# The softmax reciprocals of an attention kernel, spread over partitions by four-row products with a 0/1 matrix in place of diagonal matrices

## The chip, the core and the metric

One core of one Trainium2 chip. The metric is the device time of one execution in microseconds (us); the figure given for a kernel is the median of its runs. Engines are named as the profile names them: PE (TensorE, with PEld its weight loads), DVE (VectorE), ACT (ScalarE), POOL (GpSimd) and SP (SyncE, which issues most DMAs).

## The reference, cut to what matters

One inference step of a one-layer encoder. A projection gives two branches. Branch A is a sparse attention over 2048 positions with 8 heads of 128; its output is multiplied by a gate and goes through two further matrix products with branch B and the residual.

```python
def sparse_attention(q, qi, wi, q_pos, k, v, ki, k_pos, topk):
    ...                                  # each query keeps its top-k admissible keys
    s = jnp.einsum('bqhgd,bqkhd->bqhgk', qg, kg).astype(jnp.float32) * (HEAD_DIM ** -0.5)
    s = jnp.where(valid[:, :, None, None, :], s, -jnp.inf)
    p = jax.nn.softmax(s, axis=-1).astype(v.dtype)
    o = jnp.einsum('bqhgk,bqkhd->bqhgd', p, vg)
    return o.reshape(B, Q, ATT_W)

a_out = (o * jax.nn.silu(za)) @ w_pa
...
merged = jax.nn.sigmoid(ga) * a_out + jax.nn.sigmoid(gb) * b_out
y = x + gate[:, None, :] * (merged @ w_out)
```

The softmax divides each query's row by its sum. The kernel does that after the product with V, where the result stands with the head's 128 channels on the partitions and the queries along the free axis, so that the reciprocal of each query's sum has to be had on every partition.

## The kernel before

The program has three stages in the profiled execution: the projections (matmuls L998 to L1000, until about 1773 us), the attention (`attention()`, about 1773 to 2324 us) and the output products (`outputs()`, from there to the end). The code writes the work of each stage down in one order, and a scheduler in the program's build sets the order of the instructions on each engine from its own estimate of the times. Wide matmuls are done in three passes of f32r (an f32 form that PE reads with reduced precision): a high part of each operand (ACT's cast in `split`, L193) and what is left of it (DVE's or POOL's subtraction, L194).

The attention goes over 16 blocks of 128 queries, in the order 4, 0, 5, 1, 6, 2, 7, 3, 8 to 15; block b reads (b+1) times 128 keys. Each block has four pairs of heads, so there are 64 pairs. `qk(pr)` makes the logits of a pair (L1402 to L1404 with the weights `khi`, `klo`), adds the mask and takes the maximum (DVE, L1413), then exponentials and their sums (ACT, L1418), then the reciprocals of the sums, `sc[:, 20:22]` (DVE, L1419), one column for each of the two heads, queries on partitions. `pv(pr)` is called three pairs later. It transposes the exponentials (PE, L1439, in a PSUM tile of `ptile()`, of which there are three buffers), splits them into `th` and `tl`, and multiplies with V into the first 256 columns of `po` (L1447 to L1449). `po` has one buffer here, the same that `psi` had in the stage before.

The reciprocals get onto all partitions in `pv` as well. POOL splits them into `rr` (L1428, L1429: two high parts and two remainders), and makes from them two diagonal matrices for each part, `dg` (L1432, two instructions of 128x256 a pair). PE multiplies these with a matrix of ones, `ones_r` (L1450, L1451: two products of 256 columns), into the other 256 columns of `po`. DVE multiplies the gate `z` with these columns (L1456) and the result with the first ones (L1457), POOL makes differences (L1459 to L1461), and `xa_d` is stored (L1462).

The last `pv` is followed by a flag: PE sums it (L1869), DVE casts it to `fi` (L1871), and SP reads it (L1874, TENSOR_LOAD). `outputs()` loads pieces of the two branches from `xb_d` and `xa_d` into `xq` (L1573, five buffers, 768 KB each), of the weights into `rw` (L1553), splits both (ACT L1535 makes `xh` and `wh`, DVE L1536 `xl` and `wl`), and multiplies (L1709 to L1711). Its pool for `xq` and `xl` takes memory that the pool `ke` of the attention had, in which `khi`, `klo` and the first mask stand; a load into it waits for the last reader of what stood there.

Of the kernel before, what the change touches and what calls it, by code (L numbers as in the profile page):

```python
# [9 lines left out]
F32 = mybir.dt.float32  # L10
F32R = mybir.dt.float32r
# [3 lines left out]
ALU = mybir.AluOpType  # L15
# [4 lines left out]
P = 128  # L20
# [86 lines left out]
def body(ctx, tc, x_prompt, x_sample, cache_k, cache_v, cache_idx_k, state_conv, c_prompt, c_sample,  # L107
# [3 lines left out]
    V, S, G, T = nc.vector, nc.scalar, nc.gpsimd, nc.tensor  # L111
# [5 lines left out]
    def nm(s):  # L117
        uid[0] += 1
        return f"{s}_{uid[0]}"
# [9 lines left out]
    cp = ctx.enter_context(tc.tile_pool(name="cp", bufs=1))  # L129
# [25 lines left out]
    ident = cp.tile([P, P], F32, name="ident")  # L155
    ones = cp.tile([P, P], F32, name="ones")
    V.memset(ones, 1.0)
    ones_r = cp.tile([P, P], F32R, name="ones_r")
    V.tensor_copy(ones_r, ones)
    half = cp.tile([P, 4], F32, name="half")  # L160
    V.memset(half, -0.5)
    vecs = cp.tile([P, 96], F32, name="vecs")
# [1129 lines left out]
    def attention(shared=None, aside=()):  # L1292
        aside = list(aside)
        sums = []
        with ExitStack() as p2:
            ke = p2.enter_context(tc.tile_pool(name="ke", bufs=1, reuse_waits="tile"))
            kp = p2.enter_context(tc.tile_pool(name="kp", bufs=1, reuse_waits="tile"))
            ap_ = p2.enter_context(tc.tile_pool(name="ap", bufs=2, reuse_waits="tile"))
# [10 lines left out]
            def ptile():  # L1309
                pts[0] += 1  # L1310
                return (px if pts[0] % 3 == 0 else pst).tile([P, 512], F32, name=nm("pt"), tag="pt")
# [4 lines left out]

            khi = ke.tile([P, 2, SEQ], F32R, name="khi")
            klo = ke.tile([P, 2, SEQ], F32R, name="klo")
            mks = [ke.tile([P, SEQ], BF16, name=nm("mk"), tag="mk0")]
            vhi = kp.tile([P, NB, 256], F32R, name="vhi")  # L1320
            vlo = kp.tile([P, NB, 256], F32R, name="vlo")
# [33 lines left out]
            def block(b):  # L1355
                L = P * (b + 1)
                r0 = b * P
                st = {}
# [23 lines left out]
                def qk(pr):  # L1382

                    if pr == 0 and not st:
                        prep()
                    sc = ap_.tile([P, 32], F32, name=nm("sc"), tag="sc", bufs=5)
                    g = pr // 2
                    sms = []
                    spare = count[0] % 3 == 2 and 6 < count[0] < 60 and shared is not None
                    count[0] += 1  # L1390
                    for i in range(2):
                        if spare:
                            sm = sp.tile([P, SEQ], F32, name=nm("s"), tag=("sc", "low")[i], bufs=2 - i)
                        else:
                            sm = ap_.tile([P, SEQ], F32, name=nm("s"), tag="s", bufs=6)
                        sms.append(sm)
                        qh, ql = [t[:, 2 * (pr % 2) + i, :] for t in st["q", g]]
                        ci = 0
                        for grp in groups:
                            ps = psq.tile([P, 2, 512], F32, name=nm("ps"), tag="ps")  # L1400
                            for k, (o, w) in enumerate(grp):
                                T.matmul(ps[:, k, :w], qh, khi[:, g, o:o + w], start=True, stop=False)  # L1402
                                T.matmul(ps[:, k, :w], qh, klo[:, g, o:o + w], start=False, stop=False)  # L1403
                                T.matmul(ps[:, k, :w], ql, khi[:, g, o:o + w], start=False, stop=True)  # L1404
                            o, w = grp[0]
                            if len(grp) == 2 and grp[1][1] == w:
                                ops = [(ps[:, :, :w], o, 2, w)]
                            else:
                                ops = [(ps[:, k:k + 1, :w], o, 1, w) for k, (o, w) in enumerate(grp)]
                            for src, o, nn, w in ops:  # L1410
                                out = sm[:, o:o + nn * w].rearrange("p (a b) -> p a b", a=nn)
                                mk = st["mk"][:, o:o + nn * w].rearrange("p (a b) -> p a b", a=nn)
                                V.tensor_tensor_reduce(out, src, mk, 1.0, -3.0e38 if ci == 0 else sc[:, i * 8 + ci - 1:i * 8 + ci], ALU.add, ALU.max, sc[:, i * 8 + ci:i * 8 + ci + 1])  # L1413
                                ci += 1
                        c1 = i * 8 + ci - 1
                        r = st["r"][:, 2 * pr + i:2 * pr + i + 1]
                        V.tensor_scalar(sc[:, 16 + i:17 + i], sc[:, c1:c1 + 1], r, -1.0, ALU.mult, ALU.mult)  # L1417
                        S.activation(sm[:, :L], sm[:, :L], AF.Exp, bias=sc[:, 16 + i:17 + i], scale=r, accum_out=sc[:, 18 + i:19 + i])  # L1418
                    V.reciprocal(sc[:, 20:22], sc[:, 18:20])  # L1419
                    st[pr] = (sms, sc)  # L1420

                def pv(pr):
                    sms, sc = st.pop(pr)
                    po = pso.tile([P, 512], F32, name=nm("po"), tag="pi")
                    g = pr // 2

                    rr = ap_.tile([P, 4], F32R, name=nm("rr"), tag="rr")
                    G.tensor_copy(rr[:, 0:2], sc[:, 20:22])  # L1428
                    G.tensor_tensor(rr[:, 2:4], sc[:, 20:22], rr[:, 0:2].bitcast(F32), ALU.subtract)  # L1429
                    dg = ap_.tile([P, 2, 256], F32R, name=nm("dg"), tag="dg")  # L1430
                    for k in range(2):
                        G.tensor_tensor(dg[:, k, :].rearrange("p (i q) -> p i q", i=2), ident.unsqueeze(1).to_broadcast([P, 2, P]),  # L1432
                                        rr[:, 2 * k:2 * k + 2].bitcast(F32).unsqueeze(2).to_broadcast([P, 2, P]), ALU.mult)
                    for j0 in range(0, nj, 2):
                        js = list(range(j0, min(j0 + 2, nj)))
                        pt = ptile()
# [7 lines left out]
                        for jj, j in enumerate(js):  # L1444
# [2 lines left out]
                            T.matmul(po[:, 0:256], vh_, th[:, pc], start=(j == 0), stop=False)  # L1447
                            T.matmul(po[:, 0:256], vh_, tl[:, pc], start=False, stop=False)  # L1448
                            T.matmul(po[:, 0:256], vl_, th[:, pc], start=False, stop=(j == nj - 1))  # L1449
                    T.matmul(po[:, 256:512], ones_r, dg[:, 0, :], start=True, stop=False)  # L1450
                    T.matmul(po[:, 256:512], ones_r, dg[:, 1, :], start=False, stop=True)  # L1451
                    hs = slice(2 * pr, 2 * pr + 2)
                    z = aq.tile([P, 256], F32, name=nm("z"), tag="z", bufs=3)
                    load(z.rearrange("p (h q) -> p h q", h=2), z_d[hs, :, r0:r0 + P].rearrange("h p t -> p h t"))
# [7 lines left out]
                    store(xa_d[pr, :, :, 64 * b:64 * b + 64].rearrange("s p t -> p s t"), ps_)  # L1462

                return prep, [(lambda pr=pr: qk(pr), lambda pr=pr: pv(pr)) for pr in range(4)]

            order = [4, 0, 5, 1, 6, 2, 7, 3, 8, 9, 10, 11, 12, 13, 14, 15]
# [371 lines left out]
    def general():  # L1838
# [26 lines left out]
        outputs()  # L1865

    attention((ip, pst, psi), gates + [conv_out])
    pf = pst.tile([P, 512], F32, name="pf", tag="pt")
    T.matmul(pf[:1, 0:1], flag, ones[:, 0:1], start=True, stop=True)  # L1869
# [93 lines left out]
```

## Time and profile before

| what | us |
|---|---|
| runs | 2834.89, 2835.08, 2839.24 |
| median | 2835.08 |
| profiled execution, its own time | 2831.79 |
| its span | 2829.9 |
| mean granted PE clock | 0.992 of full speed |

The span is what the profiler's records cover, from the first instruction to the last; the execution's own time has 1.9 us around it, and stands 3.3 us below the median. Busy times of matmuls overlap (they are pipelined), so the cost of a matmul on PE is read from the distance between starts, and a row with xN holds N instructions that follow each other. In forms of PE the words 128*128 are the rows and columns of the weights in use, the rest is what is moved through and written; types of PE are all shown as f32.

### The profile page before, as it was taken

To read this page: it belongs to the slowest core of one execution; us is meant where nothing else is said; L and a number is where in the kernel's file an instruction comes from. 1 tells how busy PE (TensorE), PEld (TensorE's weight loads), DVE (VectorE), ACT (ScalarE), POOL (GpSimd) and SP (SyncE) were. 2 spreads that over 40 slices of the span, in tenths; PEclk is the share of its full clock that TensorE was granted. 3 is DMA by queue.
4 is the path that set the end of the run, shared out by engine and by line. 5 is a ranking of instruction groups with operands and counts; after the bars stand their busy time and mean duration, and the time that the engine had idled before them with its cause. 6 is when DMAs were issued, how large, how long until landed. Compare 5 with 4: busy or idle time off the path is not lost. (4 is left out here: it accounts for less than half of the span.)

```text
span 2829.9 us, 51791 instructions
## 1 busy us (share of the span) xinstructions
PE 2730.2 (96%) x18206; PEld 2636.1 (93%) x18206; DVE 2203.2 (78%) x4549; ACT 1506.2 (53%) x2719; POOL 1030.5 (36%) x1430
## 2 busy tenths in 40 slices
PE   8998899999999999999999999899999999999998
PEld 6988899999999989999999999889999999999997
DVE  6676668577778898778887855898887769887988
ACT  4433655665666754534544433676665654454453
POOL 3342646455554243222342221577554430010100
PEclk9999899999999999999999999999999999999999
DMA  8578744455454676565776775677554459896885
GB/s 292 179 241 270 244 157 162 160 170 169 158 168 162 209 195 221 180 196 187 215 222 205 224 242 164 143 198 204 152 169 147 133 186 349 253 305 208 258 295 155
DMA packets 485841, 576.29 MB, mean 204 GB/s; under 512 B 179506, under 2 KB 375298, under 8 KB 484546
## 3 DMA queue, kind: packets, MB, share of 16 engines
q1 hardware_dynamic: 476706, 556.55, 62.5%
q0 software_dynamic: 4160, 12.06, 1.2%
q10 hardware_dynamic: 4704, 4.26, 0.4%
q8 instruction: 145, 2.38, 0.4%
q14 instruction: 126, 1.03, 0.1%
HBM read 379.83 MB, written 199.22 MB: 205 GB/s over the span
## 5 line engine op out<-in xcount | busy, mean ns | idle before, releaser
L998 PE MATMUL pm<-bh,wo 128*128 128x352 f32 (+1 forms) x2688 | 865.7, 323 | 11.4 <-DVE u L1097 3.0
L999 PE MATMUL pm<-bl,wo 128*128 128x352 f32 (+1 forms) x2688 | 864.2, 322 | 0.0
L1000 PE MATMUL pm<-bh,wo 128*128 128x352 f32 (+1 forms) x2688 | 860.9, 322 | 0.0
L998 PEld LDWEIGHTS pm<-bh,wo 128*128 128x128 f32 x2688 | 507.0, 189 | 20.0 <-DVE u L1097 3.7
L999 PEld LDWEIGHTS pm<-bl,wo 128*128 128x128 f32 x2688 | 507.5, 189 | 6.1 <-issue 0.9
L1000 PEld LDWEIGHTS pm<-bh,wo 128*128 128x128 f32 x2688 | 505.5, 188 | 4.2 <-issue 0.5
L194 POOL TENSOR_TENSOR wo<-wr,wo 128x512 fp32r<-128x512 f32 x160 | 226.7, 1418 | 669.4 <-ACT wo L193 645.7
L255 DVE SCALAR_TENSOR_TENSOR sc<-pi,wi,sc 128x512 f32<-128x512 f32 (+3 forms) x287 | 192.1, 671 | 55.2 <-ACT pi L251 51.0
L251 ACT ACTIVATE pi<-pi 128x512 f32<-128x512 f32 (+3 forms) x328 | 164.7, 517 | 127.9 <-PE pi L250 120.4
L1535 ACT CAST wh<-rw 128x1024 fp32r<-128x1024 f32 x128 | 134.2, 1052 | 171.0 <-PE ps L1710 76.5
L193 ACT CAST th<-pt 128x512 fp32r<-128x512 f32 (+1 forms) x288 | 154.7, 561 | 129.7 <-PE pt L1439 116.7
L1709 PE MATMUL ps<-xh,wh 128*128 128x384 f32 (+1 forms) x672 | 214.3, 321 | 2.0 <-ACT oa L1664 0.8
L194 DVE TENSOR_TENSOR tl<-pt,th 128x512 fp32r<-128x512 f32 (+1 forms) x288 | 184.0, 655 | 40.5 <-ACT th L193 39.7
L1710 PE MATMUL ps<-xl,wh 128*128 128x384 f32 (+1 forms) x672 | 214.4, 320 | 0.0
L1711 PE MATMUL ps<-xh,wl 128*128 128x384 f32 (+1 forms) x672 | 211.6, 320 | 0.5 <-DVE wl L1536 0.5
L1536 DVE TENSOR_TENSOR wl<-rw,wh 128x1024 fp32r<-128x1024 f32 x128 | 155.5, 1221 | 50.3 <-ACT wh L1535 50.3
L1418 ACT ACTIVATE s<-s,sc,rts 128x384 f32<-128x384 f32 (+15 forms) x128 | 166.2, 1298 | 48.3 <-DVE sc L1417 36.5
L318 ACT ACTIVATE low<-sc,w 32x1056 f32<-32x1056 f32 (+14 forms) x105 | 136.6, 1301 | 87.1 <-DVE w L323 86.2
L193 ACT CAST wo<-wr 128x512 fp32r<-128x512 f32 x160 | 98.4, 615 | 140.9 <-PE pm L999 109.0
L1790 POOL DMA_DIRECT2D out_dram<-om x60 | 31.7, 534 | 388.8 <-DVE om L1788 388.8
L1063 DVE TENSOR_TENSOR u<-u,pm 128x352 f32<-128x352 f32 (+1 forms) x240 | 122.1, 510 | 58.4 <-PE pm L1000 54.6
L1447 PE MATMUL po<-th,vhi 128*128 128x256 f32 x544 | 158.7, 292 | 6.6 <-DVE a L1457 2.6
(323 smaller groups left out, 7208.1 us busy)
## 6 DMA issues: line engine op xcount, KB each, us to landing
u<-u_d SPq DMA_DIRECT2D x128, 520.0 KB, 3.7
wr<-in_w_f_dram SPq DMA_DIRECT2D x96, 512.0 KB, 4.2
rw<-o_d SPq DMA_DIRECT2D x72, 512.0 KB, 5.9
u_d<-ev SPq DMA_DIRECT2D x192, 176.0 KB, 2.5
rw<-in_w_q_dram SPq DMA_DIRECT2D x56, 512.0 KB, 6.3
s_d<-ws SPq DMA_DIRECT2D x64, 256.0 KB, 3.0
wr<-s_d SPq DMA_DIRECT2D x32, 512.0 KB, 5.1
xa_d<-a SPq DMA_DIRECT2D x64, 256.0 KB, 3.2
```

Source lines behind the costliest of these rows:

```text
L193: S.copy(hi, src)
L194: (eng or V).tensor_tensor(lo, src, hi.bitcast(F32), ALU.subtract)
L251: S.activation(pi[:n, :w], pi[:n, :w], AF.Relu)
L255: V.scalar_tensor_tensor(sc[:n, o:o + w], pi[:n, :w], wi[:n, b, h:h + 1], sc[:n, o:o + w], ALU.mult, ALU.add)
L998: T.matmul(ps[:, :tb], wh[:, kt, :], bh[:, kt, :tb], start=(first and kt == 0), stop=False, **more)
L999: T.matmul(ps[:, :tb], wh[:, kt, :], bl[:, kt, :tb], start=False, stop=False, **more)
L1000: T.matmul(ps[:, :tb], wl[:, kt, :], bh[:, kt, :tb], start=False, stop=(kt == 3), **more)
L1418: S.activation(sm[:, :L], sm[:, :L], AF.Exp, bias=sc[:, 16 + i:17 + i], scale=r, accum_out=sc[:, 18 + i:19 + i])
L1447: T.matmul(po[:, 0:256], vh_, th[:, pc], start=(j == 0), stop=False)
L1709: T.matmul(ps[:, :tb], wh[:, kt, wc], xh[:, kt, :tb], start=(first and kt == 0), stop=False, **more)
L1710: T.matmul(ps[:, :tb], wh[:, kt, wc], xl[:, kt, :tb], start=False, stop=False, **more)
L1711: T.matmul(ps[:, :tb], wl[:, kt, wc], xh[:, kt, :tb], start=False, stop=(kt == 3), **more)
```

## The change

`ones_r` and the matrices `dg` go. A matrix `pick2` of zeros and ones is made once, in the pool `ke`: for head i, rows i and i + 2 are ones. The split of the reciprocals (`rr`, POOL) moves from `pv` to the end of `qk`. In `pv`, PE transposes `rr` (128 queries by 4) into four rows of 128 in a tile of `ptile()`, ACT copies these rows to `row`, and at the end of the pair two products of 128 columns, with the first four rows of `pick2` as weights and `row` moved through, write the other 256 columns of `po`: each adds the high part and the remainder of one head.

```diff
-    ones_r = cp.tile([P, P], F32R, name="ones_r")
-    V.tensor_copy(ones_r, ones)
...
+            pick2 = ke.tile([P, 2, P], F32R, name="pick2")
+            for i in range(2):
+                V.tensor_tensor(pick2[:, i, :], ident[:, i:i + 1].to_broadcast([P, P]), ident[:, i + 2:i + 3].to_broadcast([P, P]), ALU.add)
...
                     V.reciprocal(sc[:, 20:22], sc[:, 18:20])
-                    st[pr] = (sms, sc)
+                    rr = ap_.tile([P, 4], F32R, name=nm("rr"), tag="rr", bufs=6)
+                    G.tensor_copy(rr[:, 0:2], sc[:, 20:22])
+                    G.tensor_tensor(rr[:, 2:4], sc[:, 20:22], rr[:, 0:2].bitcast(F32), ALU.subtract)
+                    st[pr] = (sms, rr)
...
-                    rr = ap_.tile([P, 4], F32R, name=nm("rr"), tag="rr")
-                    G.tensor_copy(rr[:, 0:2], sc[:, 20:22])
-                    G.tensor_tensor(rr[:, 2:4], sc[:, 20:22], rr[:, 0:2].bitcast(F32), ALU.subtract)
-                    dg = ap_.tile([P, 2, 256], F32R, name=nm("dg"), tag="dg")
-                    for k in range(2):
-                        G.tensor_tensor(dg[:, k, :].rearrange("p (i q) -> p i q", i=2), ident.unsqueeze(1).to_broadcast([P, 2, P]),
-                                        rr[:, 2 * k:2 * k + 2].bitcast(F32).unsqueeze(2).to_broadcast([P, 2, P]), ALU.mult)
+                    pr_ = ptile()
+                    T.transpose(pr_[:4, 0:P], rr.bitcast(F32), ident)
+                    row = ap_.tile([P, P], F32R, name=nm("row"), tag="row")
+                    S.copy(row[:4], pr_[:4, 0:P])
...
-                    T.matmul(po[:, 256:512], ones_r, dg[:, 0, :], start=True, stop=False)
-                    T.matmul(po[:, 256:512], ones_r, dg[:, 1, :], start=False, stop=True)
+                    for i in range(2):
+                        T.matmul(po[:, 256 + P * i:384 + P * i], pick2[:4, i, :], row[:4], start=True, stop=True)
```

PE in the middle of the attention, at the end of one pair (po is the pair's result, dg the diagonal matrices, s the exponentials). Before:

```order
L1404 MATMUL ps_23084<-khi,ql_22797 128x384
L1450 MATMUL po_23108<-dg_23112,ones_r 128x256
L1451 MATMUL po_23108<-dg_23112,ones_r 128x256
L1439 MATMUL pt_23283<-ident,s_22890 128x128
L1439 MATMUL pt_23283<-ident,s_22906 128x128
```

The same pair after (line numbers are those of the changed kernel; row holds the four rows, pick_20211 is pick2):

```order
L1447 MATMUL po_23153<-th_23208,vhi 128x256
L1431 MATMUL pt_23308<-ident,rr_22963 4x128
L1448 MATMUL po_23153<-tl_23209,vhi 128x256
...
L1449 MATMUL po_23153<-th_23221,vlo 128x256
L1451 MATMUL po_23153<-row_23156,pick_20211 128x128 x2
L1439 MATMUL pt_23327<-ident,s_22930 128x128
```

The two products of a pair still stand next to each other, in all 64 pairs, between instructions that use all 128 rows; the transposition of `rr` is an instruction more.

SP where the attention ends and `outputs()` begins. Before:

```order
L1573 DMA xq_28243<-xb_d 128x4x384
L1454 DMA z_28197<-z_d 128x2x128
L1573 DMA xq_28259<-xb_d 128x4x384
L1573 DMA xq_28265<-xb_d 128x4x384
L1462 DMA xa_d<-a_27784 128x8x64
L1573 DMA xq_28357<-xb_d 128x4x384
L1573 DMA xq_28447<-xb_d 128x4x384
L1462 DMA xa_d<-a_27923 128x8x64
L1462 DMA xa_d<-a_28061 128x8x64
L1874 TENSOR_LOAD fi
```

After:

```order
L1454 DMA z_28262<-z_d 128x2x128
L1462 DMA xa_d<-a_27855 128x8x64
L1462 DMA xa_d<-a_27992 128x8x64
L1462 DMA xa_d<-a_28128 128x8x64
L1874 TENSOR_LOAD fi
L1874 ISA x2
L1573 DMA xq_28308<-xb_d 128x4x384
L1573 DMA xq_28324<-xb_d 128x4x384
L1573 DMA xq_28330<-xb_d 128x4x384
L1573 DMA xq_28422<-xb_d 128x4x384
L1462 DMA xa_d<-a_28264 128x8x64
L1573 DMA xq_28512<-xb_d 128x4x384
```

The first five loads of `xq` stood among the last pairs' transfers and ahead of the read of the flag; now they stand behind it, since `pick2` lies in the memory that they write and is read by the very last product of the attention.

PE at the same place, after:

```order
L1449 MATMUL po_28135<-th_28250,vlo 128x256
L1451 MATMUL po_28135<-row_28138,pick_20211 128x128 x2
L1709 MATMUL ps_28347<-xh_28319,wh_28310 128x384
L1709 MATMUL ps_28362<-xh_28319,wh_28310 128x384
L1709 MATMUL ps_28376<-xh_28319,wh_28314 128x384
L1709 MATMUL ps_28390<-xh_28319,wh_28314 128x384
L1710 MATMUL ps_28347<-xl_28320,wh_28310 128x384
```

Before, L1709, L1710 and L1711 took turns from the start; now four products that need only `xh` stand ahead of the first that needs `xl`.

## Rows read from the trace of the kernel before

**Rows 1.** The page's first part: busy time of each engine, share of the span, number of instructions.
```profile
PE 2730.2 (96%) x18206; PEld 2636.1 (93%) x18206; DVE 2203.2 (78%) x4549; ACT 1506.2 (53%) x2719; POOL 1030.5 (36%) x1430
```

**Rows 2.** Busy time by stretch: two of the attention, and the first two tens of us of the output stage. The columns: the stretch and its length, then busy us (and instructions) of PE, PEld, DVE, ACT, POOL, the granted PE clock, the share of DMA time, and GB/s.
```profile
1773.00:1933.00 160.00, 145.91 (x1023) 133.18 (x1024) 138.14 (x418) 108.00 (x230) 107.77 (x279) 0.99 0.69 176
1933.00:2290.00 357.00, 355.23 (x2570) 335.33 (x2568) 289.55 (x668) 221.52 (x336) 189.31 (x397) 1.00 0.57 162
2330.00:2340.00 10.00, 10.00 (x59) 10.00 (x58) 9.46 (x12) 6.88 (x10) 0.57 (x2) 1.00 1.00 366
2340.00:2350.00 10.00, 9.83 (x56) 9.24 (x54) 4.49 (x9) 4.58 (x6) 1.07 (x2) 1.00 1.04 390
```

**Rows 3.** PE in time around the end of one pair: start in us, duration, engine, line, operation, out<-in, weights' rows*columns, what is written, count.
```profile
1789.76 0.28 PE L1449 MATMUL po<-th,vlo 128*128 128x256 f32 x1
1789.87 0.28 PE L1450 MATMUL po<-dg,ones_r 128*128 128x256 f32 x1
1789.99 0.28 PE L1451 MATMUL po<-dg,ones_r 128*128 128x256 f32 x1
1790.11 0.38 PE L1439 MATMUL pt<-ident,s 128*128 128x128 f32 x2
```

**Rows 4.** POOL from 1773 to 2330 us, the diagonal matrices and the first half of the split of the reciprocals: count, then busy us, mean ns of one, idle time before and what ended it.
```profile
L1432 POOL TENSOR_TENSOR dg<-ident,rr 128x256 fp32r<-128x256 f32 x128 | 78.3, 630 | 89.2 <-PE po L1451 78.9 <-DMA wq<-in_w_q_dram 10.2
L1428 POOL CAST rr<-sc 128x2 fp32r<-128x2 f32 x64 | 12.4, 194 | 53.5 <-DVE sc L1419 52.9
```

**Rows 5.** PE in time, matmuls that use 32 of the 128 rows of the weights (L457) between matmuls that use all of them, in the projection stage.
```profile
1683.74 0.32 PE L998 MATMUL pm<-bh,wo 128*128 128x336 f32 x1
1683.99 0.48 PE L457 MATMUL po<-sm,sm 32*128 32x128 f32 x2
1684.40 0.42 PE L999 MATMUL pm<-bl,wo 128*128 128x336 f32 x1
1684.66 0.32 PE L1000 MATMUL pm<-bh,wo 128*128 128x336 f32 x1
1684.82 0.33 PE L998 MATMUL pm<-bh,wo 128*128 128x352 f32 x1
```

**Rows 6.** PE in time, two transpositions that use 4 rows (L566) among f32r products of 256 columns.
```profile
17.42 0.28 PE L560 MATMUL pm<-wh,cs 128*4 128x256 f32 x1
17.53 0.28 PE L561 MATMUL pm<-wl,cs 128*4 128x256 f32 x1
17.74 0.28 PE L566 MATMUL pm<-ident,row 4*128 4x4 f32 x2
17.96 0.28 PE L560 MATMUL pm<-wh,cs 128*4 128x256 f32 x1
```

**Rows 7.** PE's groups by line and form: two of 256 columns that differ in type (L556 f32, L560 f32r by their declarations). Count, busy us, mean ns of one, idle time before.
```profile
L560 PE MATMUL pm<-wh,cs 128*4 128x256 f32 x40 | 9.7, 279 | 0.0
L556 PE MATMUL pm<-x,cs 128*4 128x256 f32 x16 | 3.8, 379 | 0.0
```

**Rows 8.** PE in time, f32r products of 128 columns with all rows in use (the logits of the first block).
```profile
1793.99 0.27 PE L1403 MATMUL ps<-klo,qh 128*128 128x128 f32 x1
1794.10 0.28 PE L1404 MATMUL ps<-khi,ql 128*128 128x128 f32 x1
```

**Rows 9.** PE in time, a transposition whose weights have all 128 rows and 32 columns (L451).
```profile
1741.96 0.32 PE L1000 MATMUL pm<-bh,wo 128*128 128x336 f32 x1
1742.11 0.27 PE L451 MATMUL pt<-ident,box 128*32 128x128 f32 x1
1742.22 0.60 PE L1343 MATMUL pt<-ident,s 128*128 128x128 f32 x4
```

**Rows 10.** ACT, the nearest form to the copy of the four rows: count, busy us, mean ns.
```profile
L731 ACT ACTIVATE sq<-pm 128x128 bf16<-128x128 f32 x32 | 8.9, 277 | 24.1 <-PE pm L766 19.8 <-PE pt L208 2.0 <-DVE sm L738 1.9
```

**Rows 11.** PE's groups from 1773 to 1933 us with idle time before them (last column: us, and what ended it).
```profile
L1439 PE MATMUL pt<-ident,s 128*128 128x128 f32 x272 | 40.9, 277 | 3.9 <-DVE tl L194 3.3 <-DVE sc L1413 0.2
L1447 PE MATMUL po<-th,vhi 128*128 128x256 f32 x129 | 37.7, 292 | 4.6 <-DVE a L1457 2.2 <-DVE sc L1417 1.0 <-ACT khi L193 0.7
L1451 PE MATMUL po<-dg,ones_r 128*128 128x256 f32 x28 | 7.9, 282 | 0.0
```

**Rows 12.** The end of the attention in time on SP's queue (start, time until the last of the row's transfers, count), then on ACT, DVE and PE.
```profile
2291.62 0.36 SPq L1573 DMA_DIRECT2D xq<-xb_d  x1
2296.70 1.47 ACT L1535 CAST xh<-xq 128x1536 fp32r<-128x1536 f32 x1 [0.83 <-DMA xq<-xb_d]
2298.20 1.76 DVE L1536 TENSOR_TENSOR xl<-xq,xh 128x1536 fp32r<-128x1536 f32 x1 [2.13 <-ACT xh L1535]
2323.61 0.28 PE L1451 MATMUL po<-dg,ones_r 128*128 128x256 f32 x1
2323.73 0.33 PE L1709 MATMUL ps<-xh,wh 128*128 128x384 f32 x1
2323.90 0.34 PE L1710 MATMUL ps<-xl,wh 128*128 128x384 f32 x1
```

**Rows 13.** What PE waited for from 2290 to 2313 us: waiter, releaser, us in total, times, longest.
```profile
PE po L1448 <- DVE tl L194: 1.5, 1, 1.5
PE po L1447 <- ACT th L193: 1.5, 1, 1.5
```

More of the change, by code (lines that the diff above doesn't have):

```diff
@@ L1419, in qk @@
                     V.reciprocal(sc[:, 20:22], sc[:, 18:20])
-                    st[pr] = (sms, sc)
+                    rr = ap_.tile([P, 4], F32R, name=nm("rr"), tag="rr", bufs=6)
+                    G.tensor_copy(rr[:, 0:2], sc[:, 20:22])
+                    G.tensor_tensor(rr[:, 2:4], sc[:, 20:22], rr[:, 0:2].bitcast(F32), ALU.subtract)
+                    st[pr] = (sms, rr)
                 def pv(pr):
-                    sms, sc = st.pop(pr)
+                    sms, rr = st.pop(pr)
                     po = pso.tile([P, 512], F32, name=nm("po"), tag="pi")
                     g = pr // 2
-                    rr = ap_.tile([P, 4], F32R, name=nm("rr"), tag="rr")
-                    G.tensor_copy(rr[:, 0:2], sc[:, 20:22])
-                    G.tensor_tensor(rr[:, 2:4], sc[:, 20:22], rr[:, 0:2].bitcast(F32), ALU.subtract)
-                    dg = ap_.tile([P, 2, 256], F32R, name=nm("dg"), tag="dg")
-                    for k in range(2):
-                        G.tensor_tensor(dg[:, k, :].rearrange("p (i q) -> p i q", i=2), ident.unsqueeze(1).to_broadcast([P, 2, P]),
-                                        rr[:, 2 * k:2 * k + 2].bitcast(F32).unsqueeze(2).to_broadcast([P, 2, P]), ALU.mult)
+                    pr_ = ptile()
+                    T.transpose(pr_[:4, 0:P], rr.bitcast(F32), ident)
+                    row = ap_.tile([P, P], F32R, name=nm("row"), tag="row")
+                    S.copy(row[:4], pr_[:4, 0:P])
                     for j0 in range(0, nj, 2):
```

## The prediction

> **What bounds the kernel now.** The page's shares come first: PE is busy for 96% of the span, POOL for 36% [rows 1]. A share is a mean over stages, so the next view is the busy time by stretch [rows 2]. In the attention from 1933 to 2290 us PE is busy for 355.23 of 357 us: each tenth of a microsecond that PE gets or loses there is one of the kernel. From 1773 to 1933 us, where the small blocks are done, PE is busy for 145.91 of 160 and DVE for 138.14: PE waits now and then for DVE. So the change is judged by what it does to PE. POOL, which it relieves most, is no limit: its diagonal matrices wait for PE (the 78.9 us ended by L1451 are POOL's own idle time) [rows 4], never the other way round, since L1450 follows L1449 after 0.11 us and without idle time [rows 3].
>
> **What goes.** On POOL 128 matrices at 630 ns [rows 4], 78 us: worth nothing, since nobody waits for them; DVE's instructions do not become fewer by it. On PE the two products of 256 columns: L1450, L1451 and the next instruction start at 1789.87, 1789.99 and 1790.11 [rows 3], so the two take 0.24 us a pair.
>
> **What comes, on PE.** First the transposition of `rr`, with weights of 128 rows and 4 columns. The nearest row is a transposition with 128 rows and 32 columns, which starts 0.15 us after a product of 336 columns and is followed after 0.11 us [rows 9]: 0.11 us, with no gap on either side. The products L560 with 4 columns follow each other at 0.11 to 0.12 us too [rows 6]. I take 0.11.
>
> The Trainium skill, TensorEngine Tiling (Array Packing), Key Properties, says that a change of the tiling mode drains the array, and lists modes narrow in columns beside those narrow in rows. By that rule this transposition would pay the gaps as well; the row of L451 shows none at 32 columns, and the rival "drain at both" below has that time.
>
> Then the two products, which use only four rows of weights. This trace has no f32r product of that kind. Between which rows does it lie? The **upper end** is L457: 32 rows, 128 columns, in f32. At 1683.74 an L998 of 336 columns starts, then come two L457 and an L999, and at 1684.66 the L1000 starts: 0.92 us, of which the two neighbours need 0.15 or 0.16 each (L1000 to L998: 1684.66 to 1684.82). That leaves 0.61 us for the two, where two full-row products would take 0.22 [rows 5, 8]. So the few rows cost, not the columns: a gap on entering, on leaving, and no overlap between the two. The **lower end** is L566: 4 rows, 4 columns. From L561 at 17.53 to L560 at 17.96 there are 0.43 us; L561 itself takes 0.12, which leaves 0.31 for the two [rows 6]; they move nearly nothing, so 128 columns cost more. In between: f32 moves slower than f32r, 379 against 279 ns for 256 columns [rows 7], 0.05 us for 128. L457 less twice 0.05 is **0.51 us for two f32r products**, my estimate.
>
> A pair then takes 0.51 + 0.11 instead of 0.24: **+0.38 us** (ends: 0.31 + 0.11 - 0.24 = +0.18, and +0.48). From 1933 us on there are 64 - 28 = 36 pairs (28 L1451 until then) [rows 11] on an engine without idle time: 36 x 0.38 = 13.7 us. Of the 28 before, I let a fifth go into the 14 us that PE stands anyway: 28 x 0.38 x 0.8 = 8.5. Together **+22.2 us** (ends +10.5, and +30.7 with nothing absorbed).
>
> **What comes beside PE.** ACT gets 64 copies of 4x128, at most 277 ns each [rows 10]: 18 us, where it is busy for 330 of 517 us [rows 2], off the path. But the transposed rows hold one of three PSUM tiles until ACT has copied them, 64 more users beside the tiles of exponentials; PE already waits 3.3 us for such tiles and 2.2 us for the single `po` [rows 11], and the order after leaves somewhat less PE work between a pair's products and the next pair's first L1447. For both **+2 us** (0 to 4). The two instructions for `pick2` replace one cast, once: nothing. `rr` moves from `pv` to `qk` in the code alone: POOL's idle time before L1428 is ended by the reciprocals already (52.9 of 53.5 us) [rows 4], so it does them as soon as they are there. Nothing.
>
> **The end of the attention.** SP's five loads of `xq` pass behind the flag's read and behind the last product. Before, the first was issued at 2291.62 and its split began at 2296.70, 5.08 us later; `xh` took 1.47, `xl` 1.76, long before L1709 at 2323.73, which followed the last product after 0.12 us [rows 12]. Now the load goes out when the last product is done: 5.1 + 1.5 + 1.8 = 8.4 us until the first L1710, in which only four L1709 at 0.17 us fit: PE stands for **7.7 us**. Given back are the waits of 1.5 + 1.5 us in the last pairs [rows 13]: there `xh` and `xl` sat ahead of `th` and `tl` on ACT and DVE [rows 12], and they do so no longer. Net **+4.7 us**.
>
> **Sum.** 22.2 + 2 + 4.7 = +28.9 us on the profiled execution: 2831.8 + 28.9 = 2860.7. The median stands 3.3 us above that execution: **2864 us**. Its own range by the ends of the price: +10.5 + 2 + 4.7 = +17 to +30.7 + 2 + 4.7 = +37, which is 2852 to 2872.
>
> **Rivals.**
> *Few rows cost nothing extra.* The four-row f32r products follow each other as the full ones do, 0.11 each [rows 8]: +0.09 a pair, 3.2 + 2.0 us, with 1 for waits and 4.7 at the end +11, 2846 us. Against it stand both rows with few rows; for it, that neither is f32r. The Trainium skill, TensorE: Matmul & The Clock Gate, in its section Why this matters for your kernels, says that a single matmul of 32 rows takes the time of one of 128. The starts around L457 [rows 5] speak against that here.
>
> *The five loads land together.* Issued back to back they share the bandwidth: 5 x 768 KB at some 370 GB/s (2330 to 2350 us) [rows 2] are 10.6 us, and the stretch behind them is one in which the DMA is already full (shares 1.00 and 1.04). The reads of gates and output weights stand behind them in SP's queue. If the first lands only with the last, the wait is 13.2 instead of 7.7, and the output weights come late as well: some 7 us more, 2871.
>
> *Drain at both.* The transposition pays the entering and leaving gap of L457 too, about 0.2 us: 64 x 0.2 = +12.8 on the forecast, 2877.
>
> *No difference.* The products cost by their columns, half of 0.12 each, so that a pair takes 0.12 + 0.11 against 0.24; what is left is the end of the attention, +4: 2839, inside the 0.2% (5.7 us) that a measurement of this kernel tells from nothing.
>
> *Faster.* All three new instructions are short: without gaps, at the distance at which a start of little work could follow, half of the 0.12 of a 256-column product [rows 3]. A pair then takes 0.18 against 0.24, 64 x 0.06 = -3.8, with the 3.0 us of the last pairs given back -6.8: 2828. It decides only where the wait for `xq` is nil, because the loads go out before the last product; the order of SP speaks against that, and rows 5 and 6 against the price.
>
> **How the numbers follow.** Forecast 0.60, few rows free 0.14, loads together 0.12, drain at both 0.05, no difference 0.06, faster 0.03. The range is 2845 to 2878: it takes in the first rival below and the two above; left out are no difference, faster, and the outer ends of the others. Faster by over 0.2%: 0.03; within it: 0.06; slower: 0.91, from all the rest.
>
> **What would show it.** In the profile after: starts around the two products of a pair that are 0.5 us longer than their neighbours need (0.3 to 0.6), not 0.22; the transposition at 0.11; the stretch from the 28th pair to the last one longer by about 14 us with PE still without idle time; POOL shorter by 78 us with no gain; PE standing for 7 to 8 us between the last product and the first L1710, ended by `xq`, `xh` or `xl`, and no wait for `th` and `tl` in the last pairs. The forecast is wrong if the distance between L1449 and the instruction behind the products is under 0.4 us, or if `xq` is there in time.

## The result: 28.7 us slower, and the profile after

The changed kernel took 2868.0 us in the median of its runs (2865.78 to 2873.07), the kernel before 2837.16 on the same chips. The ratio is 1.0101 (95% interval 1.0085 to 1.0117), which is +28.7 us (24 to 33); the medians alone stand 30.8 apart. A second series of the unchanged pair of kernels, among the experiments, gave 1.0109. The forecast was +28.9 and 2864.

The page of the changed kernel, its first part, which answers to [rows 1]:

```profile
PE 2763.2 (96%) x18270; PEld 2655.3 (93%) x18270; DVE 2204.3 (77%) x4550; ACT 1520.0 (53%) x2783; POOL 958.2 (33%) x1302
```

PE has 64 instructions more and is busy for 33 us more; POOL has lost 72 us, and nothing came of that. The profiled execution took 2867.1 us, 35.3 more than that of the kernel before. The new groups of PE and ACT (count, busy us, mean ns, idle time before and what ended it):

```profile
L1451 PE MATMUL po<-row,pick 4*128 4x128 f32 x128 | 27.8, 297 | 0.0
L1431 PE MATMUL pt<-ident,rr 128*4 128x128 f32 x64 | 17.3, 273 | 0.8 <-DVE tl L192 0.8
L1433 ACT CAST row<-pt 4x128 fp32r<-4x128 f32 x64 | 16.1, 252 | 19.6 <-PE pt L1431 14.7 <-PE po L1451 4.1
```

The end of one pair in time on PE, which answers to [rows 3]:

```profile
2017.90 0.28 PE L1448 MATMUL po<-tl,vhi 128*128 128x256 f32 x1
2018.02 0.28 PE L1449 MATMUL po<-th,vlo 128*128 128x256 f32 x1
2018.22 0.44 PE L1451 MATMUL po<-row,pick 4*128 4x128 f32 x2
2018.59 0.55 PE L1439 MATMUL pt<-ident,s 128*128 128x128 f32 x3
```

L1448 to L1449 is 0.12 us, as ever; L1449 to the first product is 0.20; the two products hold PE until 2018.59. Over all 64 pairs the median distances between starts are 208 ns from L1449 to the first product, 164 to the second, 201 to the instruction behind (a transposition in 52 pairs), and 165 from there to the next one. Where all rows are in use a product of 256 columns takes 116 to 118 ns and a transposition 109. So the two products take 0.738 - 0.116 - 0.109 = **0.513 us**, in place of 0.24.

The end of the attention, which answers to [rows 12]: SP's queue, then ACT, DVE and PE in time.

```profile
2349.14 2.48 SPq L1573 DMA_DIRECT2D xq<-xb_d  x4
2353.94 1.47 ACT L1535 CAST xh<-xq 128x1536 fp32r<-128x1536 f32 x1 [6.54 <-DMA xq<-xb_d]
2355.45 1.76 DVE L1536 TENSOR_TENSOR xl<-xq,xh 128x1536 fp32r<-128x1536 f32 x1 [4.89 <-ACT xh L1535]
2349.15 0.43 PE L1451 MATMUL po<-row,pick 4*128 4x128 f32 x2
2355.47 1.65 PE L1709 MATMUL ps<-xh,wh 128*128 128x384 f32 x4 [5.88 <-ACT xh L1535]
2357.26 0.69 PE L1710 MATMUL ps<-xl,wh 128*128 128x384 f32 x1
2357.75 0.52 PE L1711 MATMUL ps<-xh,wl 128*128 128x384 f32 x1
2358.07 0.52 PE L1709 MATMUL ps<-xh,wh 128*128 128x384 f32 x1
```

The loads go out with the last product, and the first L1710 starts 7.9 us behind it, where it was 0.3. Then look at the distance from L1711 to L1709: 0.32 us for 384 columns, where the trace of before has 0.17 [rows 12, L1709 to L1710].

One more wait is new, in the middle. What PE waited for from 1935 to 1960 us (waiter, releaser, us, times, longest), then the rows of ACT and PE at that place:

```profile
PE pt L1439 <- ACT row L1433: 4.3, 1, 4.3
```
```profile
1943.97 0.62 ACT L191 CAST vhi<-in 128x512 fp32r<-128x512 f32 x1 [7.32 <-DMA in<-v_d]
1944.97 0.25 ACT L1433 CAST row<-pt 4x128 fp32r<-4x128 f32 x1
1945.27 1.11 PE L1439 MATMUL pt<-ident,s 128*128 128x128 f32 x4 [4.35 <-ACT row L1433]
1947.31 0.52 PE L1404 MATMUL ps<-klo,qh 128*128 128x384 f32 x1
1947.63 0.52 PE L1405 MATMUL ps<-khi,ql 128*128 128x384 f32 x1
```

ACT stands at the split of `v`, whose load is late; the copy of the four rows is queued behind it on ACT and holds a PSUM tile; PE has no tile to transpose into. After the wait PE is slow again: 0.32 us for 384 columns. Busy time and granted clock around both places (stretch, length, busy of PE, PEld, DVE, ACT, POOL, clock, DMA share, GB/s):

```profile
1945.00:1947.00 2.00, 1.50 (x6) 0.97 (x7) 2.00 (x6) 1.27 (x4) 0.00 (x0) 0.50 0.23 39
1947.00:1950.00 3.00, 3.00 (x10) 2.94 (x11) 2.84 (x8) 1.22 (x2) 1.78 (x5) 0.50 0.53 154
1950.00:1953.00 3.00, 3.00 (x24) 2.79 (x23) 1.93 (x5) 0.84 (x4) 1.05 (x3) 0.94 0.79 199
2357.00:2360.00 3.00, 2.86 (x10) 2.74 (x10) 0.20 (x1) 0.00 (x0) 0.00 (x0) 0.51 1.04 383
2360.00:2363.00 3.00, 3.00 (x19) 3.00 (x18) 0.85 (x1) 2.31 (x4) 0.00 (x0) 1.00 1.10 346
```

After 4.4 and 5.9 us without work PE does its next 4 to 5 us of work at a granted clock of 0.50, and then the clock is back. Nine logits at 0.32 instead of 0.173 and the transpositions ahead of them make about 2.0 us at the first place, eight starts behind L1710 about 1.3 at the second. The Trainium skill, TensorE: Matmul & The Clock Gate, Part 1, tells of such a gate: half the clock after an idle window of about 3.4 us, and the full one after a busy window of the same length. Both places agree with it.

So long a wait is not needed, though. The kernel before has a stretch at half the clock as well, in its last pairs, behind the two waits of 1.5 us of [rows 13]: the stretch with the waits and the one behind it, in the same columns.

```profile
2297.00:2301.90 4.90, 1.90 (x15) 1.47 (x13) 3.55 (x4) 2.63 (x4) 0.00 (x0) 1.00 1.09 352
2301.90:2305.40 3.50, 3.50 (x19) 3.50 (x19) 1.34 (x2) 1.17 (x2) 0.00 (x0) 0.51 1.04 365
```

There 3.4 us of work ran at half the clock, products of 256 columns 0.21 us apart instead of 0.117, about 1.7 us lost, with PE busy for 1.9 of the 4.9 us ahead. In the change the waits in the last pairs are 0.7 us at the longest, and the slow stretch is not there.

Lastly the whole attention, from the first logit to the last product of a pair, in the same columns, before and after:

```profile
1773.25:2323.61 550.36, 531.66 (x3830) 497.87 (x3831) 448.40 (x1120) 346.99 (x592) 302.96 (x689) 0.99 0.60 165
1773.19:2349.30 576.11, 558.58 (x3894) 510.26 (x3895) 452.15 (x1119) 359.21 (x655) 228.17 (x561) 0.99 0.55 151
```

PE is busy for 26.9 us more, and it stands for 17.5 us where it stood for 18.7.

### The profile page after: what moved, and what is told of

It is laid out like the page before. It is cut to its first block, busy times and chain, and to the rows that moved or that the text cites. A ratio compares the mean times of both kernels' runs of the same rounds, so it can differ in the third digit from the quotient of the medians.

```text
span 2865.3 us, 51953 instructions
## 1 busy us (share of the span) xinstructions
PE 2763.2 (96%) x18270; PEld 2655.3 (93%) x18270; DVE 2204.3 (77%) x4550; ACT 1520.0 (53%) x2783; POOL 958.2 (33%) x1302
## 5 line engine op out<-in xcount | busy, mean ns | idle before, releaser
L996 PE MATMUL pm<-bh,wo 128*128 128x352 f32 (+1 forms) x2688 | 867.1, 323 | 12.4 <-DVE u L1061 3.6
L1709 PE MATMUL ps<-xh,wh 128*128 128x384 f32 (+1 forms) x672 | 215.4, 323 | 9.6 <-ACT xh L1535 5.9
L1710 PE MATMUL ps<-xl,wh 128*128 128x384 f32 (+1 forms) x672 | 215.8, 322 | 0.1
L1711 PE MATMUL ps<-xh,wl 128*128 128x384 f32 (+1 forms) x672 | 212.3, 322 | 0.5 <-DVE wl L1536 0.5
L1419 ACT ACTIVATE s<-s,sc,rts 128x640 f32<-128x640 f32 (+15 forms) x128 | 166.0, 1297 | 39.8 <-DVE sc L1418 34.0
L1439 PE MATMUL pt<-ident,s 128*128 128x128 f32 x1088 | 164.2, 276 | 6.7 <-ACT row L1433 4.9
L1448 PE MATMUL po<-tl,vhi 128*128 128x256 f32 x544 | 160.4, 295 | 2.4 <-DVE tl L192 2.1
```

The lines of the kernel that those rows point to most:

```text
L996: T.matmul(ps[:, :tb], wh[:, kt, :], bh[:, kt, :tb], start=(first and kt == 0), stop=False, **more)
L1439: T.transpose(pt[:, (2 * jj + i) * P:(2 * jj + i + 1) * P], sms[i][:, j * P:(j + 1) * P], ident)
L1709: T.matmul(ps[:, :tb], wh[:, kt, wc], xh[:, kt, :tb], start=(first and kt == 0), stop=False, **more)
L1710: T.matmul(ps[:, :tb], wh[:, kt, wc], xl[:, kt, :tb], start=False, stop=False, **more)
L1711: T.matmul(ps[:, :tb], wl[:, kt, wc], xh[:, kt, :tb], start=False, stop=(kt == 3), **more)
```

## Experiments

For each kernel: its median, the ratio to the kernel before in runs on the same chips, and three lengths worked out from the starts on PE in its one profiled execution: the attention from its first logit to the last product of a pair, from there to the first product with `xl` (L1710), and from there to the end.

| kernel | median us | ratio (95%) | attention | to L1710 | rest |
|---|---|---|---|---|---|
| before | 2835 to 2838 | 1 | 550.4 | 0.3 | 506.0 |
| the change | 2868.0 | 1.0101 (1.0085 to 1.0117) | 576.1 | 7.9 | 508.0 |
| e0, the change again | 2867.7 | 1.0109 (1.0087 to 1.0132) | 573.9 | 8.1 | 508.5 |
| e1, pick2 elsewhere | 2860.1 | 1.0087 (1.0071 to 1.0103) | 577.2 | 0.5 | 504.3 |
| e2, full rows | 2857.6 | 1.0074 (1.0057 to 1.0090) | 562.2 | 8.2 | 509.2 |
| e3, transposition alone | 2851.5 | 1.0059 (1.0041 to 1.0077) | 568.0 | 0.3 | 507.8 |
| e4, products twice | 2880.6 | 1.0152 (1.0132 to 1.0172) | 586.5 | 8.0 | 505.6 |
| e5, full rows, pick2 elsewhere | 2849.9 | 1.0042 (1.0027 to 1.0058) | 569.9 | 0.3 | 505.4 |
| e7, own tile for v | 2862.4 | 1.0093 (1.0069 to 1.0116) | 571.7 | 8.1 | 507.3 |
| e8, e5 and own tile for v | 2847.8 | 1.0036 (1.0022 to 1.0049) | 564.4 | 0.3 | 504.1 |
| e9, e8, transposed in po | 2872.9 | 1.0114 (1.0098 to 1.0130) | 588.6 | 0.3 | 507.0 |
| e10, e5, two pairs at once | 2858.8 | 1.0074 (1.0060 to 1.0088) | 573.0 | 0.3 | 504.9 |

The stage ahead of the attention, in which the edits change no more than the one cast of `ones_r`, ended and the attention began between 1772.7 and 1778.5 us in these executions, so differences of a few us between single profiles are read from the stage lengths, not from the spans.

**e1: pick2 in another pool.**

```diff
-            pick2 = ke.tile([P, 2, P], F32R, name="pick2")
+            pick2 = kp.tile([P, 2, P], F32R, name="pick2")
```

> The change with pick2 in the pool kp instead of ke, so that the first five xq loads go out before the last pairs again and ahead of the flag's read; nothing else. Theory (the end of the attention costs the change its own 6 to 8 us: in its trace PE stands 5.9 us for xh, then for xl, and runs at half the clock for some 3 us after): the wait is gone, the two waits of 1.5 us in the last pairs come back, net 5 to 7 us below the change, some 23 to 25 us above the kernel before; no stretch at clock 0.5 after the last pair. Rival (the loads only move the same DMA time): no more than 2 us below the change. Rival (the change costs through the end of the attention alone): the time of the kernel before.

It came out 7.6 us below e0 in the medians and 22.5 above the kernel before. The wait is gone; the last pair and the first output products in time on PE:

```profile
2352.58 0.44 PE L1451 MATMUL po<-row,pick 4*128 4x128 f32 x2
2352.94 0.44 PE L1709 MATMUL ps<-xh,wh 128*128 128x384 f32 x1
2353.23 0.33 PE L1710 MATMUL ps<-xl,wh 128*128 128x384 f32 x1
2353.40 0.33 PE L1711 MATMUL ps<-xh,wl 128*128 128x384 f32 x1
```

L1710 to L1711 is 0.17 again, at the full clock. What PE waited for from 2300 us to there:

```profile
PE po L1448 <- DVE tl L192: 3.4, 5, 1.5
PE po L1447 <- ACT th L191: 0.9, 1, 0.9
```

So `xh` and `xl` are in the way of `th` and `tl` once more, and from 2328.2 to 2331.6 us the last pairs have a stretch at half the clock again, as in the kernel before. The end of the attention costs the change some 4 to 8 us net (7.6 by the medians, 4 and 6 by the ratios against the two series of the change), for no reason but the pool in which a tile of 1 KB a partition lies. The mechanism is as expected; the medians lie just outside the 5 to 7 and 23 to 25 us that were expected.

**e2: the products on all rows**, and **e4: the products twice.** In e2 `row` is one of two tiles that are zeroed once:

```diff
...
-                        T.matmul(po[:, 256 + P * i:384 + P * i], pick2[:4, i, :], row[:4], start=True, stop=True)
+                        T.matmul(po[:, 256 + P * i:384 + P * i], pick2[:, i, :], row, start=True, stop=True)
```

> The change with the two products on all 128 rows: pick2 has zeros in its other rows already, row is one of two tiles zeroed once, ACT still copies four rows only. Theory (what costs is that only four rows of weights are in use): L1449 to the second instruction behind the products takes 0.45 us instead of 0.74, the two products 0.22 instead of 0.51, so 64 x 0.29 = 18.6 us below the change, 10 to 13 above the kernel before. Rival (the price comes from the order or from waits for the row copy): within 3 us of the change.

In e4 the loop over the products is `for i in (0, 1, 0, 1)`.

> The change with the two four-row products of each pair issued twice in a row (the second time writes the same). Theory (gaps on entering and leaving the four rows, 0.093 and some 0.09 once for the whole group; 0.164 from start to start within): 2 x 0.164 x 64 = 21 us above the change, about 50 above the kernel before. Rival (each four-row product pays the whole 0.26 by itself): 33 us above the change. Rival (only columns cost): 2 x 0.06 x 64 = 8 us above the change.

The end of a pair on PE, e2 first and then e4:

```profile
2023.86 0.28 PE L1454 MATMUL po<-th,vlo 128*128 128x256 f32 x1
2023.98 0.33 PE L1456 MATMUL po<-row,pick 128*128 128x128 f32 x2
2024.15 0.73 PE L1444 MATMUL pt<-ident,s 128*128 128x128 f32 x5
```
```profile
2004.35 0.28 PE L1449 MATMUL po<-th,vlo 128*128 128x256 f32 x1
2004.56 0.66 PE L1451 MATMUL po<-row,pick 4*128 4x128 f32 x4
2005.14 0.98 PE L1439 MATMUL pt<-ident,s 128*128 128x128 f32 x7
```

With all rows there is 0.12 us ahead of the products and 0.17 for both; counted as above (118 + 59 + 112 + 132 ns, less 116 and 109) they take 0.20 instead of 0.51 us. That the few rows cost is shown. In e4 the medians within the group of four are 164, 112, 112 and 200 ns: the two products more take 0.112 us each, as full ones do. 2 x 0.112 x 64 = 14.3 us, and the median rose by 12.8 over e0 (the ratios by 0.43% and 0.51%, 12 to 14 us). I had expected 21: within the group a four-row product costs nothing extra. What costs is to go into and out of the few rows: 0.513 - 2 x 0.112 = **0.29 us for a group**, whether two or four are in it (for four the same sum is 0.961 - 0.116 - 0.109 - 4 x 0.112 = 0.288).

e2's time fell by 10, not by 18.6. PE's work fell by (0.513 - 0.196) x 64 = 20 us, its attention by 11.7 to 13.9 against the change's two profiles. Most of the rest came back as waits: in the attention PE stands for 20.9 us, in the change's two profiles for 17.5 and 14.0 (for the maxima, `sc`, 8.1 us instead of 5.0, for the row copy 6.3 instead of 4.9). The half clock behind the waits is a part of it as well: PE does 12.4 us of its work in the attention at 0.50, in the change's profiles 8.0 and 12.3.

**e3: the transposition alone.** The kernel before, with

```diff
+                    pr_ = ptile()
+                    T.transpose(pr_[:4, 0:P], rr.bitcast(F32), ident)
+                    row = ap_.tile([P, 512], F32R, name=nm("row"), tag="th", bufs=5)
+                    S.copy(row[:4, 0:P], pr_[:4, 0:P])
```

> The kernel before, with the transposition of rr and ACT's copy of the four rows added (into a tile of th's tag), the result unused; the diagonal matrices and 256-column products stay. Theory (0.108 us on PE, no gap for weights narrow in columns): 64 x 0.108 = 6.9 us, with 0 to 4 us of waits for PSUM tiles and for a tile of th: 5 to 11 us above the kernel before. Rival (a gap for this mode as well, about 0.2): some 20 us above.

+13.9 us in the medians, +16.7 by the ratio (11.6 to 21.8): between the two theories. On PE the transposition takes 0.11 us here as in the change: a 256-column product behind it starts after 26 ns and takes 201, together 0.11 more than such a product's 116; another transposition starts after 109. So there is no gap, and the rival falls; 64 x 0.11 is 7.0. Of the other 7 to 10 the larger part is waits: PE stands for 23.4 us in the attention instead of 18.7, and does 10.2 us of its work at half the clock instead of 6.6, which costs 1.8. What makes up the remainder is not shown. PE's waits from 1773 to 2366 us:

```profile
PE ps L1402 <- DVE sc L1413: 8.9, 14, 2.5
PE po L1452 <- DVE tl L194: 3.8, 5, 1.5
PE pt L1443 <- DVE tl L194: 3.5, 4, 2.3
```

In the kernel before the first of these is 4.9. Whether the PSUM tile, the place in ACT's queue or the borrowed buffer of `th` does it, this kernel doesn't tell.

**e7: a tile of its own for v.**

```diff
-                vt = pair_in(v_d, j, vt)
+                if vt is not None:
+                    vt = vt[:, 256 * j:256 * j + 512]
+                else:
+                    vt = ap_.tile([P, 512], F32, name=nm("in"), tag="vin", bufs=1)
+                    load(vt.rearrange("p (j c) -> p j c", j=2), v_d[j * P:(j + 2) * P, :].rearrange("(j p) c -> p j c", p=P))
```

> The change with a tile of its own for the loads of v (L1335's second use), which so far shared two buffers with those of k and q; so the loads go out well ahead. Theory (near 1941 us ACT stands 7.3 us at vhi for v_d, the copy of the four rows is queued behind it and holds a PSUM tile, PE stands 4.4 us and then runs at half the clock for some 4 us): that wait and the slow stretch go, 5 to 6 us below the change. Rival (the row copies themselves hold PE up, whatever v does): the wait moves elsewhere, within 2 us of the change.

> The change itself, unaltered, beside the others of this chip: 28 to 31 us above the kernel before, as in its first runs. Of the two waits of its first trace, the 5.9 us for xh at the end of the attention and the 4.3 us for row near 1941 us, both theories of their cause (order of SP's queue) expect them again at the same places within 0.5 us.

e7 came out 5.3 us below e0. All that PE waited for from 1935 to 1960 us in e7:

```profile
PE pt L1435 <- DVE tl L192: 0.2, 1, 0.2
```

The wait at that place is gone, and it was due to the load. But in e0 it was 2.9 us, not the 4.3 within 0.5 that was expected (the wait for `xh` was 6.0 again), and in e7 a wait of 2.3 for a row copy stands elsewhere; the intervals of e0 and e7 overlap. I take the mechanism at that place as shown; its size, 2 to 5 us by the attention's lengths and the medians, is not settled.

**e5 and e8: the remedies together.** e5 is e1 with e2, e8 has e7's tile as well.

> Full rows and pick2 in kp together. Theory (PE's work 19 us below the change's, the end of the attention 7 to 8 below, with the waits for sc and row of the full-row kernel, some 5 us, kept): 20 to 23 us below the change, 6 to 10 above the kernel before: 64 transpositions of 0.108 on PE less 64 x 0.04, and waits. Rival (waits fill whatever PE gains): no better than the better of the two alone, some 20 above the kernel before.

> Full rows, pick2 in kp, and the own tile for v together. Theory (near 1941 us the wait for the row copy behind vhi, 5.7 us in the kernel with full rows, and the half clock after it are due to the late load of v): 5 to 7 us below full rows with pick2 in kp, which was 13.6 us above the kernel before: 6 to 9 above before remain, of which 4 are PE's work. Rival (a PE with less work only meets the next wait, on DVE): within 2 us of it.

e5 stands 13.6 us above the kernel before (ratio: 8 to 16), where 6 to 10 were expected; e8 9.7 above (ratio: 6 to 14). So e8 gained 2.1 us on e5 by the medians and 3.9 by their distances to the kernel before: between its theory (5 to 7) and its rival (within 2), and the runs do not decide. In its profile the attention is 5.6 us shorter than e5's, with 0.8 us of waits for row copies instead of 6.3. Against the kernel before, 64 x (0.11 + 0.196 - 0.24) = 4 us of the rest are PE's own work. Waits and the half clock behind them are about 6: in e8's attention PE stands for 21.5 us instead of 18.7, and does 12.5 us of its work at 0.50 instead of 6.6 (20.5 in e5). Single profiles do not split 9.7 us more finely: e8's attention is 14 us longer than that of the kernel before, whose profiled execution was one of its faster ones. What PE waited for in e8 from 1773 to 2366 us:

```profile
PE ps L1411 <- DVE sc L1422: 7.9, 8, 3.4
PE po L1457 <- DVE tl L192: 4.3, 6, 1.5
PE po L1456 <- DVE a L1466: 1.8, 6, 0.5
```

No version of the change that I ran reaches the kernel before.

**e9: transposed in po**, and **e10: two pairs at once.**

```diff
-                    pr_ = ptile()
-                    T.transpose(pr_[:4, 0:P], rr.bitcast(F32), ident)
+                    T.transpose(po[:4, 256:384], rr.bitcast(F32), ident)
...
```

> As the one with full rows, pick2 in kp and the own tile for v, but the transposed rows go into four partitions of the pair's own po instead of one of the three tiles of the exponentials. Theory (besides 0.108 us on PE a transposition costs by holding one of three tiles): no waits for row are left, 2 to 4 us lower than with the tile. Rival (the wait moves to the single po, since the first L1447 now has the transposition ahead of it in the same tile): no lower, or higher.

e9 is e8 with the transposed rows in `po`, from which ACT copies them. Its rival was right, and by more than it said: 25 us above e8. Now PE waits in `po`, which has one buffer:

```profile
PE po L1455 <- ACT row L1441: 7.2, 12, 2.8
PE pt L1447 <- DVE tl L192: 6.6, 16, 1.2
PE pt L1447 <- ACT s L1427: 4.1, 2, 3.2
```

In e10, which is e5 otherwise, `rr` holds two pairs in eight columns, and the first of the two has it transposed; `pick2` has four matrices:

```diff
...
+                    if pr % 2 == 0:
+                        pr_ = ptile()
+                        T.transpose(pr_[:8, 0:P], rr.bitcast(F32), ident)
+                        turns[0] += 1
+                        S.copy(rows_[turns[0] % 2][:8], pr_[:8, 0:P])
+                    row = rows_[turns[0] % 2]
...
```

> Full rows and pick2 in kp, with one transposition of 128x8 and one copy of eight rows for two pairs, 32 instead of 64 (pick2 has four matrices then). Theory (a transposition is 0.108 us of PE plus a share of waits): 32 x 0.108 = 3.5 us, and half of the waits for row, together 4 to 8 us below full rows with pick2 in kp, which was 13.6 us above the kernel before. Rival (PE's work alone counts): 3.5 us. Rival (what is left is the order of the loads): no change.

All three were wrong: with half the transpositions it is 9 us slower than e5. PE's waits from 1773 to 2366 us:

```profile
PE ps L1407 <- DVE sc L1418: 11.6, 15, 3.6
PE po L1455 <- DVE a L1465: 6.3, 7, 2.0
PE pt L1438 <- POOL rr L1429: 4.6, 1, 4.6
```

A pair's transposition now waits for a second pair's reciprocals, and the program's order of everything around it is another. So what the waits of the first part cost is not a price for each transposition; it depends on the order. More than that stays open.

**e6: no product at all.** The kernel before, where the transposition of the exponentials is a product with a diagonal matrix of the reciprocals:

```diff
-                                T.transpose(pt[:, (2 * jj + i) * P:(2 * jj + i + 1) * P], sms[i][:, j * P:(j + 1) * P], ident)
+                                T.matmul(pt[:, (2 * jj + i) * P:(2 * jj + i + 1) * P], sms[i][:, j * P:(j + 1) * P], dg[:, i, :], start=True, stop=True)
...
```

The kernel does without the two products, the split of the reciprocals and DVE's multiplication with the spread reciprocals.

> The kernel before without any product that spreads the reciprocals: the transposition of the exponentials (L1439) becomes an f32 product with a diagonal matrix of the reciprocals (one POOL instruction a pair, made in qk), so the exponentials come out divided by their sums, and DVE's multiplication L1456 goes. Theory: PE loses 64 x 0.24 = 15.4 us and gains 1088 x 0.002 (f32 products of 128 columns with all rows started 0.111 apart at 1666 us in the trace of before, transpositions 0.109), DVE loses 64 x 0.41: 11 to 17 us below the kernel before. Rival (an f32 product is slower than a transposition by half or more when its neighbours are f32r): 1088 x 0.05 or more, some 40 above. Rival (the transpositions now wait for POOL's matrices): near the kernel before.

2931.1 us, ratio 1.0329 (1.0305 to 1.0353): +93, on the side of the first rival. PE's group:

```profile
L1432 PE MATMUL pt<-dg,s 128*128 128x128 f32 x2176 | 291.0, 275 | 0.8 <-DVE klo L192 0.8
```

The program has 1088 such products and the trace 2176 records: an f32 product leaves two records of 0.11 us each, where the 1088 f32 transpositions of the kernel before left one each. 1088 x 0.11 = 120, less 15 for the products left out, less the 8 us that PE stands less in the attention (10.8 instead of 18.7), is 97; the attention is 98 us longer in the profile, and the run 93 by the ratio.

## Why the prediction was right, point by point

- **The sum.** +28.9 forecast, +28.7 by the ratio (24 to 33), +30.8 by the medians. The likeliest case happened, and its main term with it. That the two agree to a few tenths is luck, though. The sum was made for the profiled execution, 2860.7, and that took 2867.1: of the 35.3 us between the two profiles 25.8 are in the attention, 7.6 at its end and 2.0 behind it. The difference of the medians is smaller because the profiled execution before was 5.4 us faster than its median and the one after only 0.9.
- **The price of a pair.** 0.51 us for the two products was forecast and 0.513 measured; the transposition 0.11 and 0.11; together +0.38 a pair, 24.5 us of PE in all. The mechanism, a gap on entering the few rows and one on leaving them, is what e2 and e4 show: 0.29 us a group. The working was partly wrong, and its exact hit is luck. I took the two records of L457 [rows 5] for two products. They are one f32 product: e6 has two records for each, and in the trace of before L457 leaves 36 where the transposition of the same loop, L451, leaves 18. And of the 0.61 us around L457 0.10 lie ahead of the two records, 0.41 in them and 0.10 behind; here it is 0.09, 0.36 and 0.06. So only one of the two 0.05 that I took off for f32r lies in the products, and the other happened to be saved on leaving. "No overlap between the two" holds for the first two of a group alone: a further four-row product takes 0.112 us like any other, and for four I expected 21 us and got some 13.
- **The first 28 pairs.** I let a fifth of their price, 2.1 us, go into PE's idle time. Up to the 28th pair's last product PE stands for 13.6 us before and for 10.1 and 7.8 in the two profiles of the change, so the idle time did take up as much and more. But behind it PE stands for 5.1 us before and for 7.4 and 6.2 after, by the wait of 4.3 (2.9 in e0) us for `row`, and there is the slow clock after it, some 2.0 us; neither was in the sum as such, the 2 us for PSUM tiles stood in their place. From the first logit to the last product the attention grew by 25.8 and 23.6 us, against 21.2 in the sum (22.2 + 2 - 3.0), and the stretch from the 28th pair on by 21.0 and 19.0, where the prediction looked for about 14 and for a PE without idle time. In the end nearly the whole 24.5 us of PE's work is in the time. e2, e3 and e10 show that the waits answer to the order of everything, and no rule of a fifth holds for them.
- **The end of the attention.** 7.7 us of standing were forecast; the first L1710 comes 7.6 us later behind the last product than before. The load to the split took 4.8 us (5.1 expected). Of the two waits of 1.5 us [rows 13] less came back than thought, since waits for `tl` of 1.4 us in all remained in the last pairs. The clock was in the sum on neither side: 1.7 us at half the clock behind those two waits were given back, and 1.3 behind the new wait came on top. That makes 7.6 - 3.0 + 1.4 - 1.7 + 1.3 = 5.6 us, and e1 gives some 4 to 8, where 4.7 were forecast.
- **POOL.** Its matrices, 78 us, were worth nothing, as said: POOL is busy for 72 us less, and PE does not gain by it.
- **Rivals.** "Few rows cost nothing extra" falls for a group of two by e2, which took 20 us off PE. The Trainium skill says in TensorE: Matmul & The Clock Gate, Why this matters for your kernels, that a single matmul of 32 rows takes the time of one of 128. For the four rows of this case that holds only inside a group, by the 0.112 us of e4. "The five loads land together" did not happen: the first was there after 4.8 us. "Drain at both" falls by the 0.11 us that the transposition takes (e3). "No difference" and "faster" needed a cheap pair, and it was not.

## What to carry to other kernels

Behind another of its kind, a product that uses only four of the 128 rows took what a full one takes (0.112 us), but going in and out of the few rows cost 0.29 us for each group here; where the other rows can hold zeros, use all of them, or put such matmuls together. Work taken from an engine nobody waits for is worth nothing, while the pool of one small tile was worth some 4 to 8 us here: see which loads into that memory now wait for the new tile's last reader. When waits of PE come or go, look in the trace for the stretches at half the clock behind them, and count these as well, before and after; two waits of 1.5 us were enough for one here.

## What had not been expected of the hardware

- An f32 product leaves two records on PE and takes 0.22 us for 128 columns with all rows in use (e6), twice the f32 transposition's 0.109; I had read the two as two instructions.
- Entering and leaving four rows costs 0.29 us a group (0.513 less 2 x 0.112), with 0.112 us for each further product inside (e4).
- After 4.4 and 5.9 us without work, PE did its next 4 to 5 us of work at a granted clock of 0.50, with products of 384 columns 0.32 us apart instead of 0.17. In the kernel before, two waits of 1.48 and 1.52 us within 3.4 us were followed by 3.4 us at 0.51.
